# One of eight input tiles in a buffer of its own, at another address, and 31 activation buffers

## The chip, the cores and the metric

The kernel runs on one core of one Trainium2 chip. The metric is the device time of one execution in microseconds. Three executions took 1576.14, 1582.8 and 1582.92 us, a median of 1582.8 us.

## The reference

A trunk of four residual layers over 256 positions with 1024 channels. Layer 0 and 3 mix tokens by a dilated sliding-window attention with three head groups, layer 1 by a gated short convolution, layer 2 by a Conformer convolution module. Every layer ends in a gated convolutional feed-forward block of width 2816. Each sub-layer has a norm before and one after it:

```python
for i in range(DEPTH):
    a = rms_norm(h, mix_norm_pre[i])
    m = mixer[i % 3](a)                    # attention, short conv, conformer, attention
    h = h + rms_norm(m, mix_norm_post[i])
    f = conv_ffn(rms_norm(h, ffn_norm_pre[i]), ffn_w_in[i], ffn_w_conv[i], ffn_w_out[i])
    h = h + rms_norm(f, ffn_norm_post[i])

def conv_ffn(x, w_in, w_conv, w_out):      # w_in 1024 x 5632, w_out 2816 x 1024
    g, v = jnp.split(causal_dwconv(x @ w_in, w_conv), 2, axis=-1)
    return (jax.nn.silu(g) * v) @ w_out
```

All values are float32.

## The kernel before, in words

Channels lie on the 128 partitions and the 256 positions along the free dimension, so an activation of 1024 channels is eight tiles of 128 x 256. A matrix product keeps float32 accuracy by splitting both operands into a high and a low part of the type fp32r: `mm3` (L279 to L282) issues three matmuls for one 128 x 128 block of weights, high weights with the high input, high weights with the low input, low weights with the high input. Each matmul loads 128 columns of weights (the profile's engine PEld) and streams 256 columns of input (engine PE). A column (`column`, L462) is eight such triples, one for each input tile k, into one half of a PSUM bank: 24 matmuls. The first four columns of a stage are issued tile by tile (`ramp`, L433 to L440), since the tiles come one after the other. `value` (L878 to L880) is the attention's other form: there the input tile is the loaded operand, in halves of 128 positions, and the weights stream.

Weights come from HBM in blocks of 1 MB on SP's queue; ScalarE makes the high part (L192) and VectorE the low part (L198), in rings of 11 buffers each. In a feed-forward block 40 columns follow the ramp, and between them stand slabs (`Slabs`, L522): 14 of 24 matmuls each, and eight tails of 24, which multiply gated outputs with the second weight matrix. The short convolution has 20 columns and 192 slab matmuls after its ramp, the Conformer 12 columns, an attention layer 48 columns and 12 values of 48 matmuls. The first column after a ramp carries a hook before tile k = 3 (`if hook and k == 3`, L465): four small matmuls that spread the norm's factor (L324) stand there.

The eight input tiles are made in `boundary` (L341) once for each sub-layer, eight times in all. `hi(k)` takes a buffer by `two()` (L265) and ScalarE writes the high part into its first half (1024 bytes in each partition), `lo(k)` lets VectorE write the low part into the second half. `two()` hands out one of `NACT` equal buffers of 2048 bytes, the pool's tag "act", in turn; nearly all other activations come from the same ring. Ahead of the ring the pool holds a tile of 448 bytes, "gap" (L236), that nothing uses; it moves what comes behind it.

Where the buffers lie in a partition follows from the sizes. Every block of high or low weights begins 32 bytes past a multiple of 512. Every high part and every low part of the ring begins 480 bytes past one (162272 is the ring's first address), so the streamed operand lies 448 bytes, or minus 64, from the loaded one, counted modulo 512. In `value` the operands are swapped, and the distance is plus 64. At the step from a value to a column, and back, one matmul streams from the same place modulo 512 from which the next weights are loaded: distance 0. Such a step is called a crossing below.

The order of the work on each engine is fixed by the order in which the program issues it, and no scheduler changes it.

Of the kernel before, what the change touches and what calls it, by code (L numbers as in the profile page):

```python
# [11 lines left out]
F32R = mybir.dt.float32r  # L12
# [4 lines left out]
P = 128  # L17
D = 1024
T = 256
# [12 lines left out]
BIG = 1e30  # L32
HKF = KF // 2
SLOTS = 11
NACT = 32
PE_TAPS = (13, 13, 13, 15)
SPLIT = 60
FIRST = 10
# [190 lines left out]
def trunk_kernel(ctx: ExitStack, tc: tile.TileContext, xT, pos, params, consts, masks, w8, out):  # L229
# [4 lines left out]
    ap = ctx.enter_context(tc.tile_pool(name="ap", bufs=1))  # L234
    ps = ctx.enter_context(tc.tile_pool(name="ps", bufs=1, space=bass.MemoryType.PSUM))
    ap.tile([P, 112], F32, tag="gap", name="gap")  # L236

    st = Stream(nc, rawp, wp, SLOTS, 3, [w8[i] for i in range(w8.shape[0])])
    for _, _, _, nk, _, cols in plan():
# [15 lines left out]
    def pc(name, k):  # L255
        o, n = PCOLS[name]
        return par[:, o + k:o + k + 1]

    counter = [0]

    def act(dt=F32, tag="act", bufs=NACT, shape=(P, 2, T)):
        counter[0] += 1
        return ap.tile(list(shape), dt, tag=tag, name=f"{tag}{counter[0]}", bufs=bufs)

    def two():  # L265
        t = act(F32R)
        return t[:, 0, :], t[:, 1, :]

    def tmp():
        return act(F32, "tmp", 9, (P, T))  # L270
# [13 lines left out]
    def TT(out, a, b, op):  # L284
        nc.vector.tensor_tensor(out=out, in0=a, in1=b, op=op)  # L285

    def STT(out, a, s, b, op0, op1):
        nc.vector.scalar_tensor_tensor(out=out, in0=a, scalar=s, in1=b, op0=op0, op1=op1)  # L288

    def scaled(out, a, s, b=0.0):  # L290
        nc.scalar.activation(out=out, in_=a, func=AF.Identity, scale=s, bias=b)  # L291

    def perm(a):
        return a.rearrange("p (i j) -> p j i", j=4)
# [22 lines left out]
    def add_eps(out, a, b, eps):  # L317
        STT(out, a, eps * D / P, b, ALU.add, ALU.add)
# [19 lines left out]
    def bc2(a):  # L338
        return a.rearrange("p (s t) -> p s t", s=1).to_broadcast([P, 2, T])

    def boundary(mg, rb, gain, permuted=False):  # L341


        xs = [None] * KD

        def hi(k):
            x = two()
            src = perm(h[k]) if permuted else h[k]
            v = [a.rearrange("p (j i) -> p j i", j=4) for a in x] if permuted else x
            scaled(v[0], src, pc(gain, k))  # L350
            xs[k] = x, v, src

        def lo(k):
            x, v, src = xs[k]
            STT(v[1], src, pc(gain, k), v[0].bitcast(F32), ALU.mult, ALU.subtract)
            xs[k] = x

        sq = []

        def square(q):  # L360
            s = act()
            if permuted:
                for e in range(2):
                    nc.scalar.activation(out=s[:, e, :].rearrange("p (j i) -> p j i", j=4), in_=perm(h[2 * q + e]),
                                         func=AF.Square)
            else:
                nc.scalar.activation(out=s, in_=h2[q], func=AF.Square)
            sq.append(s)

        NP = KD // 2  # L370
        if mg is None:
            for q in range(NP):
                for k in (2 * q, 2 * q + 1):
                    hi(k)
                if q == 0:
                    st.copy()
                for k in (2 * q, 2 * q + 1):
                    lo(k)
                if q == 0:
                    st.diff()  # L380
            for q in range(NP):
                st.copy()
                square(q)
                st.diff()
            st.copy()
            st.diff()
        elif not gain:
            for q in range(NP):
                TT(mg[q], mg[q], bc2(rb), ALU.mult)
                if q:  # L390
                    TT(h2[q - 1], h2[q - 1], mg[q - 1], ALU.add)
                    nc.sync.dma_start(out=out[q - 1], in_=h2[q - 1])
            TT(h2[NP - 1], h2[NP - 1], mg[NP - 1], ALU.add)
            nc.sync.dma_start(out=out[NP - 1], in_=h2[NP - 1])
        else:
            for e in range(2):
                TT(mg[0][:, e, :], mg[0][:, e, :], rb, ALU.mult)
            for e in range(2):
                TT(h[e], h[e], mg[0][:, e, :], ALU.add)
                hi(e)  # L400
            for q in range(1, NP):
                TT(mg[q], mg[q], bc2(rb), ALU.mult)
                lo(2 * q - 2)
                lo(2 * q - 1)
                TT(h2[q], h2[q], mg[q], ALU.add)
                hi(2 * q)
                hi(2 * q + 1)
                square(q - 1)
            lo(KD - 2)
            lo(KD - 1)  # L410
            square(NP - 1)
        if not gain:
            return None, None
        a = sq[0]
        for s in sq[1:]:
            TT(a, a, s, ALU.add)
        acc = tmp()
        add_eps(acc, a[:, 0, :], a[:, 1, :], EPS_RMS)
        return xs, acc
# [137 lines left out]
    def ffn(l, mg, rb):  # L557
# [5 lines left out]
        def gate(last=False):  # L563

            ts = pend.pop(0)
            TT(ts[1], ts[0], ts[1], ALU.mult)
            x = two()
            nc.scalar.copy(out=x[0], in_=ts[1])
            st.diff()
            TT(x[1], ts[1], x[0].bitcast(F32), ALU.subtract)  # L570
            st.copy()
            gs.append(x)
# [41 lines left out]
    def short_conv(l, mg, rb):  # L614
# [10 lines left out]
        for what, k in sc_steps():  # L625
            if what == "col":
# [12 lines left out]
                TT(y, b, rb, ALU.mult)  # L639
                TT(y, y, u, ALU.mult)  # L640
                x = two()
                nc.scalar.copy(out=x[0], in_=y)
                between()
# [558 lines left out]
```

## Time and profile before

| | us |
|---|---|
| median of three executions | 1582.8 |
| profiled execution | 1583.57 |
| its span | 1581.7 |
| TensorE (PE) busy | 1555.7 (98%) |
| VectorE (DVE) busy | 1243.0 (79%) |
| ScalarE (ACT) busy | 925.2 (58%) |

The profiled execution spent 1.87 us outside the span. Each matmul's row has a start and a modelled length; matmuls overlap, so the pace of TensorE is the distance from one start to the next and not the length.

### The profile page before, as it was taken

The numbers are of one execution on the slowest core, as the hardware profiler recorded it, in microseconds if no ns is written. First come the engines' busy times: TensorE is split into PE (matmuls) and PEld (weight loads), VectorE is DVE, ScalarE is ACT, GpSimd is POOL, SyncE is SP. The second block draws the span as 40 slices with busy tenths as digits, with TensorE's granted clock in tenths as the row PEclk, the third lists the DMA queues.
The fourth block names the chain that finished last, engine by engine and source line by source line (L and its number), as shares of the span: only waits on it lengthen the run. The fifth ranks groups of instructions, "written<-read, shape, count | busy, mean of one in ns | idle before, by whom it ended". The sixth has DMA issues, their size and how long they took to land.

```text
span 1581.7 us, 31426 instructions
## 1 busy us (share of the span) xinstructions
PE 1555.7 (98%) x13146; PEld 1520.5 (96%) x13146; DVE 1243.0 (79%) x2177; ACT 925.2 (58%) x1623; POOL 17.9 (1%) x51
## 2 busy tenths in 40 slices
PE   6999999999999999999999999999999999999998
PEld 6999999999999999999999999999999999999997
DVE  4997877697876779889599598786887778588783
ACT  6564655575564566656477666565655445566562
POOL 4000000000000000000000000000000000000000
PEclk9999999999999999999999999999999999999999
DMA  5653543265552644655243136554453434236540
GB/s 218 216 212 131 176 145 108 99 232 204 187 190 100 217 161 162 238 187 184 110 144 124 54 118 239 197 174 153 178 192 138 161 134 160 107 134 237 190 160 28
DMA packets 36718, 256.94 MB, mean 162 GB/s; under 512 B 4320, under 2 KB 4448, under 8 KB 5984
## 3 DMA queue, kind: packets, MB, share of 16 engines
q1 hardware_dynamic: 36288, 254.93, 45.0%
q8 instruction: 103, 1.69, 0.4%
q14 instruction: 39, 0.32, 0.1%
q10 hardware_dynamic: 288, 0.01, 0.0%
HBM read 253.87 MB, written 1.05 MB: 161 GB/s over the span
## 4 chain that ended last, share of the span: by engine, by line
PE 93%; DVE 3%; ACT 1%; POOL 1%; issue 1%; DMA 1%; DVEq 0%; ACTq 0%; POOLq 0%
PE psA L522 17%; PE psB L282 10%; PE psB L280 10%; PE psB L281 10%; PE psA L280 7%; PE psA L281 7%; PE psA L282 7%; PE psA L878 3%; PE psA L880 3%; PE psA L879 3%; PE psB L715 2%; PE psB L926 2%; PE psB L897 2%; PE psA L438 2%; PE psB L915 2%; PE psA L433 2%
## 5 line engine op out<-in xcount | busy, mean ns | idle before, releaser
L198 DVE TENSOR_TENSOR wlo<-raw,whi 128x1024 fp32r<-128x1024 f32 x480 | 580.7, 1221 | 35.3 <-ACT whi L192 34.4
L192 ACT CAST whi<-raw 128x1024 fp32r<-128x1024 f32 x480 | 490.9, 1048 | 23.8 <-DMA raw<-in_w_dram 18.7
L282 PE MATMUL psB<-act,wlo 128*128 128x256 f32 x1392 | 390.7, 281 | 0.0
L280 PE MATMUL psB<-act,whi 128*128 128x256 f32 x1392 | 390.7, 281 | 0.0
L281 PE MATMUL psB<-act,whi 128*128 128x256 f32 x1392 | 390.7, 281 | 0.0
L280 PE MATMUL psA<-act,whi 128*128 128x256 f32 x1040 | 299.2, 288 | 8.0 <-ACT whi L192 7.1
L282 PE MATMUL psA<-act,wlo 128*128 128x256 f32 x1040 | 290.7, 280 | 0.5 <-DVE wlo L198 0.5
L281 PE MATMUL psA<-act,whi 128*128 128x256 f32 x1040 | 290.8, 280 | 0.2
L522 PE MATMUL psA<-act,whi 128*128 128x256 f32 x1536 | 272.9, 281 | 0.0
L281 PEld LDWEIGHTS psB<-act,whi 128*128 128x128 f32 x1392 | 265.0, 190 | 0.0
L282 PEld LDWEIGHTS psB<-act,wlo 128*128 128x128 f32 x1392 | 263.1, 189 | 0.0
L280 PEld LDWEIGHTS psB<-act,whi 128*128 128x128 f32 x1392 | 261.3, 188 | 0.0
L522 PEld LDWEIGHTS psA<-act,whi 128*128 128x128 f32 x1536 | 236.2, 189 | 0.0
L522 PE MATMUL psA<-act,wlo 128*128 128x256 f32 x768 | 215.8, 281 | 0.0
L280 PEld LDWEIGHTS psA<-act,whi 128*128 128x128 f32 x1040 | 196.9, 189 | 12.8 <-ACT whi L192 7.1
L282 PEld LDWEIGHTS psA<-act,wlo 128*128 128x128 f32 x1040 | 197.1, 190 | 0.8 <-DVE wlo L198 0.8
L281 PEld LDWEIGHTS psA<-act,whi 128*128 128x128 f32 x1040 | 197.2, 190 | 0.6 <-DVE act L285 0.5
L291 ACT ACTIVATE tmp<-act,par 128x256 f32<-128x256 f32 x176 | 80.2, 503 | 167.5 <-DVE act L285 167.5
L288 DVE SCALAR_TENSOR_TENSOR tmp<-act,par,tmp 128x255 f32<-128x255 f32 (+1 forms) x352 | 146.7, 480 | 19.7 <-ACT tmp L291 19.7
L522 PEld LDWEIGHTS psA<-act,wlo 128*128 128x128 f32 x768 | 145.2, 189 | 0.0
L285 DVE TENSOR_TENSOR act<-psB,act 128x512 f32<-128x512 f32 (+2 forms) x94 | 58.5, 626 | 89.1 <-PE psB L282 52.2
L878 PE MATMUL psA<-whi,act 128*128 128x256 f32 x384 | 111.0, 289 | 0.0
(124 smaller groups left out, 2116.1 us busy)
## 6 DMA issues: line engine op xcount, KB each, us to landing
raw<-in_w_dram SPq DMA_DIRECT2D x239, 1024.0 KB, 4.8
h<-in_xT_dram SPq DMA_DIRECT2D x4, 256.0 KB, 5.0
raw<-in_w_dram SPq DMA_DIRECT2D x2, 512.0 KB, 5.5
out_dram<-h SPq DMA_DIRECT2D x4, 256.0 KB, 2.0
msk<-in_masks_dram SPq DMA_DIRECT2D x1, 512.0 KB, 9.3
par<-in_params_dram SPq DMA_DIRECT2D x1, 484.0 KB, 10.0
cst<-in_consts_dram SPq DMA_DIRECT2D x1, 132.0 KB, 5.9
par<-in_params_dram ACTq DMA_DIRECT2D x1, 4.0 KB, 2.9
```

The source lines that it names most:

```text
L192: self.nc.scalar.copy(out=hi, in_=raw)
L198: self.nc.vector.tensor_tensor(out=lo, in0=raw, in1=hi.bitcast(F32), op=ALU.subtract)
L280: nc.tensor.matmul(o, lhsT=whi, rhs=x[0], start=first, stop=False)
L281: nc.tensor.matmul(o, lhsT=whi, rhs=x[1], start=False, stop=False)
L282: nc.tensor.matmul(o, lhsT=wlo, rhs=x[0], start=False, stop=last)
L285: nc.vector.tensor_tensor(out=out, in0=a, in1=b, op=op)
L288: nc.vector.scalar_tensor_tensor(out=out, in0=a, scalar=s, in1=b, op0=op0, op1=op1)
L291: nc.scalar.activation(out=out, in_=a, func=AF.Identity, scale=s, bias=b)
L522: nc.tensor.matmul(o, lhsT=a, rhs=b, start=first and i == 0, stop=last and i == 2, skip_group_check=True)
L878: nc.tensor.matmul(oc, lhsT=xh, rhs=whi[:, k % 4, :], start=k == 0, stop=False)
L879: nc.tensor.matmul(oc, lhsT=xh, rhs=wlo[:, k % 4, :], start=False, stop=False)
L880: nc.tensor.matmul(oc, lhsT=xl, rhs=whi[:, k % 4, :], start=False, stop=k == KD - 1)
```

## The change

`boundary` passes the tile's number to `two`, and for k = 3 `two` hands out the two halves of a tile "apart", made once for the whole program between "gap" and the ring. The other seven tiles come from the ring as before, which now has 31 buffers.

```
-NACT = 32
+NACT = 31
+ODD = 3
...
     ap.tile([P, 112], F32, tag="gap", name="gap")
+    apart = ap.tile([P, 2 * T + 32], F32R, tag="apart", name="apart")
...
-    def two():
+    def two(k=None):
+
+        if k == ODD:
+            return apart[:, 16:16 + T], apart[:, 288:288 + T]
         t = act(F32R)
         return t[:, 0, :], t[:, 1, :]
...
         def hi(k):
-            x = two()
+            x = two(k)
```

What this does to addresses: "apart" is 2176 bytes long, 128 more than a ring buffer, and stands ahead of the ring, so all of the ring moves to 96 bytes past a multiple of 512. The low part of tile 3 (1152 bytes into "apart") begins there too. Its high part (64 bytes into "apart") begins at 32, which is 64 bytes past the ring's old place, 64 bytes short of its new one, and the same as the weights' place. The streamed operand of a column now lies plus 64 bytes from the loaded one, modulo 512, and 0 bytes for the high part of tile 3; in a value it is minus 64, and 0.

Every engine issues the same instructions in the same order as before, and every wait of TensorE, VectorE, GpSimd and the queues is the same. Eight waits of ScalarE for its own earlier instructions are different.

## Rows read from the trace of the kernel before

**Rows 1.** The page: busy engines, granted clock in 40 slices.
```profile
PE 1555.7 (98%) x13146; PEld 1520.5 (96%) x13146; DVE 1243.0 (79%) x2177; ACT 925.2 (58%) x1623; POOL 17.9 (1%) x51
...
PEclk9999999999999999999999999999999999999999
```
**Rows 2.** The page's chain of waits, shares of the span by engine.
```profile
PE 93%; DVE 3%; ACT 1%; POOL 1%; issue 1%; DMA 1%; DVEq 0%; ACTq 0%; POOLq 0%
```
**Rows 3.** TensorE's longest waits: total us, times, longest.
```profile
PE psA L280 <- ACT whi L192: 7.1, 1, 7.1
...
PE psA L282 <- DVE wlo L198: 0.5, 1, 0.5
```
**Rows 4.** Four of six stretches: length, each engine's busy time (instructions), granted clock, DMA.
```profile
311.00:484.00 173.00, 173.00 (x1471) 173.00 (x1470) 142.57 (x226) 107.42 (x170) 0.00 (x0) 1.00 0.56 201
503.00:580.00 77.00, 77.00 (x656) 77.00 (x655) 60.27 (x92) 45.76 (x72) 0.00 (x0) 1.00 0.60 217
...
886.00:904.00 18.00, 18.00 (x161) 18.00 (x160) 9.36 (x15) 15.21 (x28) 0.00 (x0) 1.00 0.17 59
...
1397.00:1569.00 172.00, 172.00 (x1462) 172.00 (x1462) 134.34 (x219) 99.70 (x161) 0.00 (x0) 1.00 0.46 166
```
**Rows 5.** Groups by line, 311 to 484 us (feed-forward of layer 0): count, busy, mean ns.
```profile
L280 PE MATMUL psB<-act,whi 128*128 128x256 f32 x288 | 80.9, 281 | 0.0
...
L522 PE MATMUL psA<-act,whi 128*128 128x256 f32 x348 | 61.8, 281 | 0.0
```
**Rows 6.** The same view, 884 to 904.8 us (second half of the Conformer).
```profile
L280 PE MATMUL psB<-act,whi 128*128 128x256 f32 x32 | 8.8, 276 | 0.0
```
**Rows 7.** Timeline of TensorE, first value to column: start us, length, line.
```profile
46.20 0.28 PE L878 MATMUL psA<-whi,act 128*128 128x256 f32 x1
...
46.43 0.28 PE L880 MATMUL psA<-whi,act 128*128 128x256 f32 x1
46.55 0.28 PE L280 MATMUL psA<-act,whi 128*128 128x256 f32 x1
46.67 0.28 PE L281 MATMUL psA<-act,whi 128*128 128x256 f32 x1
46.78 0.28 PE L282 MATMUL psA<-act,wlo 128*128 128x256 f32 x1
46.90 0.28 PE L280 MATMUL psA<-act,whi 128*128 128x256 f32 x1
```
**Rows 8.** The same, column to value, 45 starts later.
```profile
52.00 0.28 PE L878 MATMUL psA<-whi,act 128*128 128x256 f32 x1
...
52.79 0.28 PE L879 MATMUL psA<-wlo,act 128*128 128x256 f32 x1
```
**Rows 9.** The same, value to column again.
```profile
57.10 0.28 PE L878 MATMUL psA<-whi,act 128*128 128x256 f32 x1
...
57.33 0.28 PE L880 MATMUL psA<-whi,act 128*128 128x256 f32 x1
57.44 0.28 PE L280 MATMUL psA<-act,whi 128*128 128x256 f32 x1
57.56 0.28 PE L281 MATMUL psA<-act,whi 128*128 128x256 f32 x1
...
57.80 0.28 PE L280 MATMUL psA<-act,whi 128*128 128x256 f32 x1
```
**Rows 10.** Groups by line, attention of layer 0, 62 to 287 us.
```profile
L281 PE MATMUL psA<-act,whi 128*128 128x256 f32 x340 | 94.5, 278 | 0.1
...
L879 PE MATMUL psA<-wlo,act 128*128 128x256 f32 x144 | 40.1, 279 | 0.0
```
**Rows 11.** The same, attention of layer 3, 1114 to 1366 us.
```profile
L281 PE MATMUL psA<-act,whi 128*128 128x256 f32 x381 | 105.7, 277 | 0.1
...
L879 PE MATMUL psA<-wlo,act 128*128 128x256 f32 x192 | 53.5, 278 | 0.0
```

## The prediction

> **What bounds the kernel now.** The page comes first: TensorE is busy for 98% of the span [rows 1] and carries 93% of the chain of waits [rows 2]. Its longest wait for another engine is one of 7.1 us at the start, and for weights from VectorE it waits 0.5 us in all [rows 3]. So the time is the number of matmuls times the distance from one start to the next. [...]
>
> The next view is the busy time by stretches. It also counts matmuls that began up to 0.28 us before the stretch, so 0.28 us are added. From 311 to 484 us, in the feed-forward of layer 0, it is (173.00 + 0.28) / 1471 = 117.8 ns from start to start; from 886 to 904 us, in the Conformer, (18.00 + 0.28) / 161 = 113.5 ns [rows 4]. These are the same instruction forms with no wait among them. The groups by line show it too: a mean length of 281 ns in the one stretch and 276 ns in the other [rows 5, 6]. I call them the long and the short pace. Short convolution, 503 to 580 us, and layer 3's feed-forward, 1397 to 1569 us, run at the long one [rows 4]; so do the two feed-forwards in between.
>
> The timeline shows where the pace changes without a wait. At 46 us a value ends and a column begins, a crossing in the sense given above: starts lie 0.12 us apart until 46.78 us, then 46.90 us begins a run [rows 7] that reaches 52.00 us after 45 starts, 5.10 / 45 = 113.3 ns [rows 8]. At 52.00 us a column gives way to a value, again over a distance of 0, and the pace stays: 46.90 to 52.79 us is 52 starts, 5.89 / 52 = 113.3 ns, so this crossing costs under 2 ns. At 57.44 us a value gives way to a column, and the pace turns from short (57.10 to 57.44 us, 3 starts) to long (57.44 to 57.80 us, 3 starts in 0.36 us) [rows 9]. So at equal addresses both paces hold themselves, and what turns one into the other, with no wait near, is a step in the distance between streamed and loaded addresses.
>
> **The change, part by part.** Nothing is added, removed or moved in order, so the only direct terms are buffers and addresses.
>
> *31 buffers.* The ring turns over one buffer sooner, but tile 3 no longer takes one. No wait of TensorE or VectorE changes, and eight of ScalarE change toward its own, earlier work, which is done when it gets there. Cost 0; ScalarE, busy 58% [rows 1], covers it, and eight waits of even one cast could not add 8 us.
>
> *Tile 3's high part.* In each column the distance now goes 64, 0, 64, 0, 64 around tile 3: two crossings where there was none. Columns whose input comes from `boundary`: 160 in four feed-forwards, 20, 12, and 96 in two attentions, with 24 values beside them, some 310. I read the crossing as a push that ends the long pace, as at 46.78 us, and leaves the short one, as at 52.00 us. Per matmul that is 117.8 - 113.3 = 4.5 ns. The terms:
> - Feed-forward: 40 columns, 14 slabs and 8 tails of 24 are 1488 matmuls, four times 5952, 26.8 us. Slabs have no odd tile; they keep the pace of the column before, as the short one was kept for 45 starts across two columns [rows 7, 8].
> - Short convolution: 480 + 192 = 672, 3.0 us. Conformer's first half: 288, 1.3 us.
> - Attention: mean lengths of 278 and 279 ns in layer 0, between 276 and 281, make 0.4 of 3 x 340 column matmuls and 0.6 of 3 x 144 value matmuls long; 277 and 278 in layer 3 make 0.2 of 3 x 381 and 0.4 of 3 x 192 [rows 10, 11]. That is 408 + 259 + 229 + 230 = 1126. Transposes break these columns up, and tile 3 comes late in each, so half: 563, 2.5 us.
>
> Together 33.6 us. Against it 310 x 2 crossings at under 2 ns [rows 8], 1.2 us at most, of which I take 1.0. Next in line is VectorE: 142.57 of 173 us in a feed-forward [rows 4] become 142.57 of 166.4, 86%, still under TensorE; I take 1.0 us for low weights that come late, which is twice what all such waits are now [rows 3]. Net 31.6 us, from the profiled execution's 1583.6 us: 1552 us. That execution lies 0.8 us above the median.
>
> *The new distance, plus 64.* A value runs at it now, at 279 ns on average in layer 0 against the columns' 278 [rows 10]. Both paces exist there too, the short one from 52.00 to 57.44 us [rows 8, 9]. I give the steady pace at it no price; the bounds are the two paces.
>
> *A steady distance of 0.* The first four columns of each stage use tile 3's high part eight times in a row against weights at distance 0. The trace has only single steps of it: 0.12 us between starts at 46.55 to 46.78 us [rows 7], like the long pace, and under 0.115 us at 52.00 us [rows 8]. Over 8 stages x 8 matmuls the difference is 64 x 4.5 ns = 0.3 us either way, which I leave out.
>
> **The rivals.**
>
> *No effect.* The pace is set by something other than addresses, and the long one stays. For it: 1471 starts in a row keep it through columns and slabs [rows 4, 5]; and a crossing can leave a pace as it is [rows 8]. Against it: the two others above turn it. It gives 1583 to 1586 us, the upper end if 310 x 2 crossings cost 4 ns each, the difference between 0.12 and 0.116 us, 2.5 us. [...]
>
> *Half of it.* The push works in both directions, so every second column is long, as a value's end made one pace short at 46.78 us and the other long at 57.44 us [rows 7, 9]. Half of 33.6 us, 16.8, less 1.0: about 1568 us.
>
> *Slower.* The crossing out of the short pace decides: in each column tile 3 throws it into the long pace, as at 57.44 us, and nothing brings it back. Its place is the two attentions, where the short pace has 0.6 x 1020 + 0.4 x 432 + 0.8 x 1143 + 0.6 x 576 = 2045 matmuls, 9.2 us, and crossings at 4 ns add 2.5 us: 1595 us. From 60% of those matmuls on it is slower by more than a measurement can miss ((7.9 - 2.5) / 9.2 us).
>
> **How the numbers follow.** The outcome hangs on two questions: does the push end the long pace (at 46.78 us it did), and does it spare the short one (at 52.00 us it did, at 57.44 us it did not). I give the forecast 0.35, half of it 0.17, no effect 0.23, slower 0.25. A measurement can tell 0.5%, 7.9 us, from no change: below 1574.9 us is faster, above 1590.7 us slower. The first two cases are faster, 0.52; no effect is within, 0.23; the rest slower, 0.25. The forecast's own range is 1547 (the other half of the attention, 2.5 us, and no price for crossings and VectorE) to 1561 us (a third of the feed-forward stays long, 8.9 us). The range reaches to the other cases: 1546 to 1596 us.
>
> **What would show it.** Right: the stretches of the feed-forwards show a mean length of 276 ns where 281 stood, some 1488 matmuls in 168.6 us, and slabs in step with the columns; within the first column behind a ramp the starts close up to 0.113 us from tile 3 on. Wrong: 281 ns in the feed-forwards, or a mean above it. Half: a mean near 278.5 ns, with columns that alternate. The slower rival shows in the attentions, with lengths of 281 ns where 277 and 278 stood. If TensorE then waits for low weights by several us, VectorE was nearer than I put it.

## The result, and the profile after

The changed kernel takes 1593.33 us (median of four executions, 1592.70 to 1593.88). The kernel before took 1582.86 us beside it (four executions, 1576.14 to 1583.16). The ratio is 1.0081, with a 95% interval of 1.0056 to 1.0105. Ratios below leave out one execution of experiment 8, which lasted 8732.95 us. The forecast of 1552 us was wrong; the time lies where the rival "slower" put it, at 1595 us.

The profiled execution took 1593.88 us, with a span of 1592.0 us. Three rows of the page of the changed kernel answer to [rows 1], and its shares of the chain of waits to [rows 2]:

```profile
PE 1565.4 (98%) x13146; PEld 1529.7 (96%) x13146; DVE 1243.6 (78%) x2177; ACT 924.9 (58%) x1623; POOL 18.5 (1%) x51
...
PEclk9999999999999999999999999999999999999999
...
PE 95%; DVE 2%; POOL 1%; ACT 1%; DMA 1%; issue 0%; DVEq 0%; ACTq 0%; POOLq 0%
```

The same 13146 matmuls are busy for 9.7 us more at the same granted clock (0.997 on average, 0.996 before), while VectorE and ScalarE stand where they were. The two waits of TensorE of [rows 3] have not grown (total us, times, longest; a line stands up to five further down than before). Another at the start, for ScalarE, went from 4.8 to 5.5 us:

```profile
PE psA L285 <- ACT whi L193: 7.0, 1, 7.0
PE psB L1093 <- ACT act L1084: 5.5, 1, 5.5
...
PE psA L287 <- DVE wlo L199: 0.5, 1, 0.5
```

So most of the loss must be in the distance between starts. The stretches of [rows 4], moved along by what the program is late there (length, busy time and count of PE, PEld, DVE, ACT, POOL, clock, DMA):

```profile
311.00:484.00 173.00, 173.00 (x1472) 173.00 (x1471) 142.01 (x230) 107.76 (x170) 0.00 (x0) 1.00 0.55 196
503.00:580.00 77.00, 77.00 (x657) 77.00 (x656) 59.73 (x95) 43.30 (x65) 0.00 (x0) 1.00 0.56 205
888.00:906.00 18.00, 18.00 (x153) 18.00 (x154) 8.72 (x17) 15.26 (x28) 0.00 (x0) 1.00 0.04 5
1407.00:1579.00 172.00, 172.00 (x1463) 172.00 (x1462) 134.64 (x219) 99.69 (x162) 0.00 (x0) 1.00 0.47 166
```

In the feed-forwards and the short convolution the counts are those of before: the long pace has stayed, 1472 matmuls against 1471 in 173 us. In the Conformer 161 have become 153: what ran at the short pace there now runs at the long one. The groups by line say the same for the Conformer's second half, 887 to 907 us, where [rows 6] had 276 ns, and for the attentions of layer 0 (62 to 290 us) and layer 3 (1122 to 1376 us), where [rows 10, 11] had 278 and 277 ns for the columns and 279 and 278 for the values (count, busy, mean ns):

```profile
L285 PE MATMUL psB<-act,whi 128*128 128x256 f32 x22 | 6.2, 280 | 0.0
```
```profile
L286 PE MATMUL psA<-act,whi 128*128 128x256 f32 x303 | 84.8, 280 | 0.1
...
L884 PE MATMUL psA<-wlo,act 128*128 128x256 f32 x126 | 35.3, 280 | 0.0
```
```profile
L286 PE MATMUL psA<-act,whi 128*128 128x256 f32 x338 | 94.6, 280 | 0.1
...
L884 PE MATMUL psA<-wlo,act 128*128 128x256 f32 x168 | 47.1, 280 | 0.0
```

The timeline of TensorE shows what happens inside an attention's column (start us, length; "apart" is tile 3):

```profile
110.28 0.28 PE L287 MATMUL psA<-act,wlo 128*128 128x256 f32 x1
...
110.95 0.28 PE L287 MATMUL psA<-act,wlo 128*128 128x256 f32 x1
111.07 0.28 PE L285 MATMUL psA<-apart,whi 128*128 128x256 f32 x1
111.19 0.28 PE L286 MATMUL psA<-apart,whi 128*128 128x256 f32 x1
111.31 0.28 PE L287 MATMUL psA<-apart,wlo 128*128 128x256 f32 x1
111.43 0.28 PE L285 MATMUL psA<-act,whi 128*128 128x256 f32 x1
...
112.01 0.28 PE L287 MATMUL psA<-act,wlo 128*128 128x256 f32 x1
```

From 110.28 to 110.95 us there are 6 starts in 0.67 us, 112 ns each: the short pace. From 111.07 to 111.43 us there are 3 in 0.36 us, 120 ns. From 111.43 to 112.01 us there are 5 in 0.58 us, 116 ns, and from there to its end the column keeps the long pace. Tile 3 has thrown the column out of the short pace, and nothing has brought it back.

The engines issue the same instructions in the same order, so both traces can be laid over each other matmul by matmul, and the time from the start of one to the start of another compared:

| stretch (starts) | before, us | after, us | |
|---|---|---|---|
| each of four feed-forwards from the hook on (1478) | 174.08 | 174.07 | 0.0 |
| short convolution from the hook on (662) | 77.97 | 77.97 | 0.0 |
| layer 0: first columns, then the attention | 39.45 + 223.41 | 39.83 + 226.16 | +3.1 |
| layer 3: the attention | 246.74 | 250.45 | +3.7 |
| two attentions' output columns | 11.45 + 11.56 | 11.90 + 12.01 | +0.9 |
| Conformer, second half | 21.08 | 21.95 | +0.9 |
| six ramps with the column behind each, up to the hook | | | +1.3 |

These are 9.9 of the 10.3 us between the two profiled executions. Most of the rest lies in the small matmuls between the Conformer's two halves, where in both traces the granted clock is at 0.5 for 3.4 us: 10.11 us became 10.68. The 0.4 us of the first columns lie in a stretch that holds the longer wait for ScalarE, so they are not clearly tile 3's or the ring's.

### The profile page after: what moved, and what is told of

The parts are those of the page before. It is cut to its first block, busy times and chain, and to the rows that moved or that the text cites. A ratio compares the mean times of both kernels' runs of the same rounds, so it can differ in the third digit from the quotient of the medians.

```text
span 1592.0 us, 31425 instructions
## 1 busy us (share of the span) xinstructions
PE 1565.4 (98%) x13146; PEld 1529.7 (96%) x13146; DVE 1243.6 (78%) x2177; ACT 924.9 (58%) x1623; POOL 18.5 (1%) x51
## 3 DMA queue, kind: packets, MB, share of 16 engines
HBM read 253.87 MB, written 1.05 MB: 160 GB/s over the span
## 4 chain that ended last, share of the span: by engine, by line
PE 95%; DVE 2%; POOL 1%; ACT 1%; DMA 1%; issue 0%; DVEq 0%; ACTq 0%; POOLq 0%
PE psA L527 17%; PE psB L286 10%; PE psB L285 10%; PE psB L287 10%; PE psA L285 8%; PE psA L286 7%; PE psA L287 7%; PE psA L883 3%; PE psA L884 3%; PE psA L885 3%; PE psB L720 2%; PE psB L902 2%; PE psB L931 2%; PE psA L443 2%; PE psB L920 2%; PE psA L438 2%
## 5 line engine op out<-in xcount | busy, mean ns | idle before, releaser
L286 PE MATMUL psB<-act,whi 128*128 128x256 f32 x1230 | 344.7, 280 | 0.0
L285 PE MATMUL psB<-act,whi 128*128 128x256 f32 x1230 | 344.2, 280 | 0.0
L287 PE MATMUL psB<-act,wlo 128*128 128x256 f32 x1230 | 343.3, 279 | 0.0
L285 PE MATMUL psA<-act,whi 128*128 128x256 f32 x918 | 265.3, 289 | 7.9 <-ACT whi L193 7.0
L527 PE MATMUL psA<-act,whi 128*128 128x256 f32 x1536 | 272.9, 280 | 0.0
L287 PE MATMUL psA<-act,wlo 128*128 128x256 f32 x918 | 257.5, 280 | 0.5 <-DVE wlo L199 0.5
L286 PE MATMUL psA<-act,whi 128*128 128x256 f32 x918 | 257.7, 281 | 0.2
L527 PEld LDWEIGHTS psA<-act,whi 128*128 128x128 f32 x1536 | 234.4, 188 | 0.0
L285 PEld LDWEIGHTS psB<-act,whi 128*128 128x128 f32 x1230 | 231.4, 188 | 0.0
L286 PEld LDWEIGHTS psB<-act,whi 128*128 128x128 f32 x1230 | 231.0, 188 | 0.0
L287 PEld LDWEIGHTS psB<-act,wlo 128*128 128x128 f32 x1230 | 230.3, 187 | 0.0
L527 PE MATMUL psA<-act,wlo 128*128 128x256 f32 x768 | 214.3, 279 | 0.0
L285 PEld LDWEIGHTS psA<-act,whi 128*128 128x128 f32 x918 | 173.5, 189 | 12.7 <-ACT whi L193 7.0
L286 PEld LDWEIGHTS psA<-act,whi 128*128 128x128 f32 x918 | 173.6, 189 | 0.6 <-DVE act L290 0.5
L287 PEld LDWEIGHTS psA<-act,wlo 128*128 128x128 f32 x918 | 172.9, 188 | 0.9 <-DVE wlo L199 0.8
L527 PEld LDWEIGHTS psA<-act,wlo 128*128 128x128 f32 x768 | 143.6, 187 | 0.0
L911 ACT ACTIVATE act<-act,tiny 128x512 f32<-128x512 f32 x64 | 46.4, 725 | 110.6 <-DVE tiny L909 110.6
```

Of the source, the lines that this page charges most:

```text
L285: nc.tensor.matmul(o, lhsT=whi, rhs=x[0], start=first, stop=False)
L286: nc.tensor.matmul(o, lhsT=whi, rhs=x[1], start=False, stop=False)
L287: nc.tensor.matmul(o, lhsT=wlo, rhs=x[0], start=False, stop=last)
L527: nc.tensor.matmul(o, lhsT=a, rhs=b, start=first and i == 0, stop=last and i == 2, skip_group_check=True)
```

## The experiments

Each is the changed kernel or the kernel before with one edit. "Distance" is streamed minus loaded address, modulo 512, as in the prediction; it is minus 64 in the kernel before, plus 64 in the changed one, and 0 for tile 3's high part. Three theories stand behind experiments 4 to 7; T, D, S and C stand in the expectations themselves. L: what counts is where a step of the distance lands; a step that lands on minus 64 ends the long pace, one that lands on plus 64 ends the short one. Z: what counts is that the distance is 0 at some matmul of the column. A: what counts is the alignment of the buffers, and not their distance. Unless said otherwise a stretch of 320 to 470 us lies in the feed-forward of layer 0; in the kernel before it holds 1276 matmuls, and 1326 would be the short pace throughout:

```profile
320.00:470.00 150.00, 150.00 (x1276) 150.00 (x1275) 127.09 (x202) 93.79 (x145) 0.00 (x0) 1.00 0.59 211
```

**1. The ring's move alone.** Tile 3 comes from the ring again; "apart" stays in its place, unused.

```
-            x = two(k)
+            x = two()
```

> All eight input tiles from the ring, which stays at its new place, plus 64 bytes from the weights modulo 512; 31 buffers. Theory T (tile 3's crossing throws the short pace into the long one, and nothing brings it back): the crossing is gone, so the short pace comes back in the attentions, the ramps and the second half of the Conformer: 1583 us. Theory D (at plus 64 the ring's own distance loses the short pace): 1593 us, as with the whole change, with a mean length of 281 ns in the second half of the Conformer.

Measured: 1589.26 us, ratio 1.0045 (1.0029 to 1.0060), between the 1583 us of T and the 1593 us of D. The feed-forward is long as before:

```profile
320.00:470.00 150.00, 150.00 (x1276) 150.00 (x1275) 127.47 (x203) 93.62 (x145) 0.00 (x0) 1.00 0.58 210
```

Laid over the kernel before, layer 0's attention is 1.4 us longer and layer 3's 1.5, the output columns 0.9, the Conformer's second half 0.8 and the ramps 1.2. So about 6 of the 10.5 us come with the ring at plus 64 with no odd tile at all. Of the other 4, 3.6 are tile 3's, in the attentions: they lose 2.9 us here and 6.5 in the changed kernel (both without the first columns). The small matmuls at the low clock (0.5), which lose 0.6 us in the changed kernel, lose none here.

**2. The tile alone.** The ring goes back to minus 64, since "apart" is now 2560 bytes long; tile 3's high part stays at distance 0, its low part at minus 64.

```
-    apart = ap.tile([P, 2 * T + 32], F32R, tag="apart", name="apart")
+    apart = ap.tile([P, 2 * T + 128], F32R, tag="apart", name="apart")
...
-            return apart[:, 16:16 + T], apart[:, 288:288 + T]
+            return apart[:, 16:16 + T], apart[:, 384:384 + T]
```

> Tile 3 in a buffer of its own with its high part at distance 0, and the ring at its old place, minus 64. T: in the attentions each column turns long at tile 3, 1590 to 1592 us; the Conformer's second half and the first four output columns of the attentions, which have no such tile, keep the short pace. D: 1583 us, attentions as before.

Measured: 1559.64 us, ratio 0.9852 (0.9837 to 0.9867). T and D expected no gain, and both missed. The push of the forecast is there, at a ring that stands at minus 64. Its first column behind a ramp in layer 0, tile 3 and then the end:

```profile
311.46 0.36 PE L285 MATMUL psA<-apart,whi 128*128 128x256 f32 x1
311.66 0.28 PE L286 MATMUL psA<-apart,whi 128*128 128x256 f32 x1
311.78 0.28 PE L287 MATMUL psA<-apart,wlo 128*128 128x256 f32 x1
311.90 0.28 PE L285 MATMUL psA<-act,whi 128*128 128x256 f32 x1
...
312.61 0.28 PE L285 MATMUL psA<-act,whi 128*128 128x256 f32 x1
...
313.29 0.28 PE L285 MATMUL psA<-act,whi 128*128 128x256 f32 x1
```

From 311.66 to 311.90 us two starts take 0.24 us; from 312.61 to 313.29 us six take 0.68 us, 113 ns. Ahead of the hook this column's starts are 118 ns apart. In the four feed-forwards, the short convolution and the Conformer's first half, six stages, it is the same: long up to tile 3, short within nine starts from it. The pace stays short to the end of the layer, in the slabs too (2299 of 2304 slab distances):

```profile
320.00:470.00 150.00, 150.00 (x1317) 150.00 (x1316) 129.63 (x207) 96.72 (x151) 0.00 (x0) 1.00 0.59 211
```

It is 1317 and not 1326, because each column pays for its step to 0 and back: the starts around tile 3 are 119, 118, 118, 122, 116 and 114 ns apart, 27 ns over six short ones. The attentions gain nothing, +0.5 and +0.8 us.

**3. 31 buffers alone**, in the kernel before.

```
-NACT = 32
+NACT = 31
```

> Only 31 buffers in place of 32, every address as before modulo 512. Both theories: 1583 us, within 0.5%. If it is slower by several us, the shorter ring costs by itself.

Measured: 1583.55 us, ratio 0.9999 (0.9990 to 1.0008). The buffers cost nothing. One thing in its trace is a warning: here too the Conformer's second half is long, 21.95 us, at minus 64. So which pace that stretch falls into is not the distance's alone, and I count its 0.9 us in the changed kernel as not explained.

**4. Alignment.** In the kernel before, 32 bytes ahead of the weights move weights and activations alike: everything lies on a multiple of 64 bytes, and the distance between them does not change. One other distance does: the hook streams an identity matrix from the constants, which stay where they were.

```
+    cp.tile([P, 8], F32, name="pad")
```

> The kernel before with all weights and activations moved by 32 bytes together, so that they begin on multiples of 64 bytes; their distance modulo 512 is unchanged. If only the distance counts (D and T): 1583 us, paces of 113.3 and 117.8 ns. [...]

Measured: 1567.21 us (1561.46 to 1571.22), ratio 0.9887 (0.9867 to 0.9907), and not 1583 us. A would have shown as a pace shorter than the short one, and there is none: it is 113.34 and 117.78 ns as before. The gain is whole feed-forwards that fall into one or the other. Of layer 0 to 3:

```profile
320.00:470.00 150.00, 150.00 (x1276) 150.00 (x1275) 127.11 (x203) 93.75 (x145) 0.00 (x0) 1.00 0.58 211
610.00:760.00 150.00, 150.00 (x1326) 150.00 (x1325) 130.60 (x208) 98.33 (x153) 0.56 (x5) 1.00 0.61 218
925.00:1075.00 150.00, 150.00 (x1326) 150.00 (x1325) 131.78 (x209) 98.70 (x153) 0.00 (x0) 1.00 0.60 217
1395.00:1545.00 150.00, 150.00 (x1275) 150.00 (x1275) 122.28 (x198) 89.33 (x141) 0.00 (x0) 1.00 0.50 181
```

Behind the hook layers 1 and 2 are short and stay so for all 1478 starts, 6.56 us less each; layers 0 and 3 stay long. In these two kernels without an odd tile a feed-forward's pace is settled at the hook, and not by the pace ahead of it: here layers 1 and 2 are long ahead of the hook, and in the kernel before three of the four feed-forwards are short ahead of it (113.3 to 113.4 ns) and long behind it (117.8 ns). So at one distance, minus 64 bytes, a stage can fall into either pace with no step at all. Whether it is the hook's own distance or the 32 bytes as such that turned layers 1 and 2 isn't shown. This kernel's executions differ by up to 10 us; one feed-forward more or less is 6.6, which is also how far the lowest execution of the kernel before (1576.14 us) lies under its median. That this is the reason there was not traced.

**5 and 6. Other steps that land on minus 64.** The layout of experiment 2, with tile 3's high part at plus 64, and at minus 128, instead of 0.

```
+            return apart[:, 32:32 + T], apart[:, 384:384 + T]
```
```
+            return apart[:, 112:112 + T], apart[:, 384:384 + T]
```

> Ring at its old place (minus 64 modulo 512); tile 3's high part at plus 64 instead of 0. Theory Z (it is distance 0 that pushes: streamed and loaded operand in the same place): no push, the feed-forwards stay at 117.8 ns, 1583 to 1592 us. Theory L (it is the landing on minus 64, from any other distance, that leaves the short pace behind): as with tile 3 at 0, feed-forwards at about 114 ns, 1560 us.

> Ring at its old place; tile 3's high part 64 bytes on the other side, at minus 128. Z: no push, 1583 to 1592 us. L: 1560 us. If it lands near 1560 us while plus 64 does not, the direction of the step counts.

Measured: 1557.27 us, ratio 0.9845 (0.9818 to 0.9872), and 1563.49 us, ratio 0.9884 (0.9857 to 0.9912). First the one, then the other:

```profile
320.00:470.00 150.00, 150.00 (x1322) 150.00 (x1321) 130.06 (x207) 97.04 (x152) 0.00 (x0) 1.00 0.59 213
```
```profile
320.00:470.00 150.00, 150.00 (x1315) 150.00 (x1315) 130.28 (x206) 96.89 (x150) 0.00 (x0) 1.00 0.59 211
```

Both end the long pace in the feed-forwards, and in neither is an operand of a column at distance 0. Z falls: it isn't 0 that counts. From plus 64 the push is less sure: in five of six stages the first column stays long behind tile 3, and only the second column's tile 3 ends the long pace. So with the ring at minus 64 an odd tile at any of three distances ends the long pace. The price differs too: the feed-forward takes 168.15 us from plus 64, 168.59 from 0 and 168.84 from minus 128, against 167.55 without a step (experiment 8), which is 15, 26 and 32 ns for each of 40 columns.

**7. The mirror.** The ring at plus 64, as in the changed kernel, with tile 3's high part at minus 64.

```
-            return apart[:, 16:16 + T], apart[:, 288:288 + T]
+            return apart[:, 0:T], apart[:, 288:288 + T]
```

> Ring at its new place (plus 64) as in the changed kernel; tile 3's high part at minus 64, so that a triple goes 64, -64, 64, -64, 64. L: the columns land on plus 64, where no step has yet brought the short pace: 1593 us. Z: there is no distance 0 in a column: the ring's cost alone, 1589 us.

Measured: 1588.39 us, ratio 1.0044 (1.0026 to 1.0062), level with experiment 1. The feed-forward stays long:

```profile
320.00:470.00 150.00, 150.00 (x1277) 150.00 (x1276) 127.24 (x202) 93.83 (x146) 0.00 (x0) 1.00 0.59 210
```

A step that lands on plus 64 does not end the long pace, from minus 64 here or from 0 in the changed kernel. But tile 3 does end the short one, as L had it. One of the attention's columns:

```profile
46.29 0.28 PE L285 MATMUL psA<-act,whi 128*128 128x256 f32 x1
...
47.31 0.28 PE L285 MATMUL psA<-apart,whi 128*128 128x256 f32 x1
...
47.67 0.28 PE L285 MATMUL psA<-act,whi 128*128 128x256 f32 x1
...
48.37 0.28 PE L285 MATMUL psA<-act,whi 128*128 128x256 f32 x1
```

From 46.29 to 47.31 us nine starts take 1.02 us, 113 ns; from 47.67 to 48.37 us six take 0.70 us, 117 ns. That the time is level with experiment 1 all the same, and not at the 1593 us of L, is two effects that cancel: the attentions are 1.4 and 2.1 us longer than before, against 1.4 and 1.5 with no odd tile, since their columns run longer (117.3 ns on average, against 116.5 and 116.1 in experiment 1) and their values shorter (114.8 and 114.7 ns, against 116.2 and 116.0).

The traces hold 273 columns that read tile 3 and have no hook. Counted by the pace ahead of tile 3 and the pace at the column's end:

| kernel | ring at | tile 3's high part at | long ahead: turn short | short ahead: turn long |
|---|---|---|---|---|
| before | -64 | -64 | 0 of 205 | 0 of 68 |
| experiment 2 | -64 | 0 | 16 of 20 | 0 of 253 |
| experiment 5 | -64 | 64 | 21 of 40 | 0 of 233 |
| experiment 6 | -64 | -128 | 11 of 21 | 0 of 252 |
| experiment 1 | 64 | 64 | 0 of 245 | 0 of 28 |
| changed | 64 | 0 | 0 of 263 | 10 of 10 |
| experiment 7 | 64 | -64 | 0 of 250 | 23 of 23 |

So at minus 64 tile 3 ends the long pace, though not every time, and never the short one; at plus 64 it ends the short pace every time, and never the long one. Without an odd tile no column turns. Tile 3's distance is left and come back to twice in a column, so which of the steps does it, out or back, no run tells apart. The misses at minus 64 are in part all eight Conformer columns behind other matmuls (L715 in the kernel before) in experiments 5 and 6; why is open.

**8. One step in each stage, from a second copy.** The ring at minus 64 and all of tile 3 in it; a second copy of its high part, at distance 0, is read only by the ramp and the first column behind it in feed-forwards, short convolution and Conformer. ScalarE writes one copy more in these six stages. The core of the edit, against the changed kernel:

```
-    apart = ap.tile([P, 2 * T + 32], F32R, tag="apart", name="apart")
+    apart = ap.tile([P, 384], F32R, tag="apart", name="apart")[:, 16:16 + T]
...
+            if k == ODD and not permuted:
+                v = apart, x[1]
...
+        if not permuted:
+            scaled(xs[ODD][0], h[ODD], pc(gain, ODD))
...
+    def odd(xs):
+        return xs[:ODD] + [(apart, xs[ODD][1])] + xs[ODD + 1:]
...
-                    column(xs, o, hook)
+                    column(odd(xs) if hook else xs, o, hook)
```

> Ring at its old place; a second copy of tile 3's high part at distance 0, used only in the ramp and in the one column after the hook, in feed-forwards, short convolution and Conformer; none in the attentions; one more cast on ScalarE for each of six stages. If one landing is enough and the pace then keeps itself: feed-forwards at 113.3 ns without the 27 ns that each further crossing cost, 4 x 6.5 + 2.9 + 1.2 = 30 us under before, 1553 us. If the pace does not keep itself over columns and slabs without a crossing in each: 1570 us or more.

Measured: 1554.8 us, ratio 0.9827 (0.9808 to 0.9846). It is the fastest kernel of the study, 28 us under the kernel before:

```profile
320.00:470.00 150.00, 150.00 (x1326) 150.00 (x1325) 130.17 (x206) 97.28 (x151) 0.00 (x0) 1.00 0.60 216
```

The steps of one tile in one column are enough, and the extra copy isn't what does it, since experiment 2 has none and turns at the same place. Every feed-forward then runs all its 1478 starts at 113.36 ns, 6.5 us less in each, and the short convolution 2.9 us less. Again the Conformer's second half fell into the long pace, +0.8 us.

**9 to 12. A steady distance.** The kernel before with another length of "gap" (in floats), so that all of the ring stands at distance 0, 256, minus 128 and minus 32.

```
-    ap.tile([P, 112], F32, tag="gap", name="gap")
+    ap.tile([P, 128], F32, tag="gap", name="gap")
```

with 64, 96 and 120 in the three others.

> The kernel before, its ring moved so that all streamed inputs lie at distance 0 from the weights modulo 512 and no tile stands apart. Theory S (the two paces, 113.3 and 117.8 ns, hold themselves at any distance, and the distance only decides which one a start falls into): both paces and no third, feed-forwards at one of the two, 1555 to 1592 us. Theory C (streams in the same place delay each other): a longer pace than 117.8 ns, over 1600 us.

> The same with all streamed inputs at plus 256, as far as they can be modulo 512. S: both paces, 1555 to 1592 us. C: the short pace everywhere, 1545 to 1555 us.

> The same with all streamed inputs at minus 128. S: both paces, 1555 to 1592 us. If distance counts only modulo 128, as distance 0: the time of that kernel within 2 us.

> The kernel before with all streamed inputs at minus 32, half way between distance 0 (120.0 ns from start to start) and minus 64 (113.3 or 117.8 ns). If the pace changes smoothly with the distance, between these: 117 to 120 ns in the feed-forwards, 1585 to 1605 us. [...]

Measured: 1615.96 us, ratio 1.0226 (1.0175 to 1.0276); 1616.26 us, 1.0228 (1.0176 to 1.0279); 1603.10 us, 1.0144 (1.0094 to 1.0195); 1597.75 us, 1.0088 (1.0059 to 1.0117). The stretch in the four, in this order:

```profile
320.00:470.00 150.00, 150.00 (x1253) 150.00 (x1252) 129.56 (x212) 92.80 (x145) 0.00 (x0) 1.00 0.56 198
```
```profile
320.00:470.00 150.00, 150.00 (x1253) 150.00 (x1252) 129.55 (x211) 92.77 (x146) 0.00 (x0) 1.00 0.56 197
```
```profile
320.00:470.00 150.00, 150.00 (x1267) 150.00 (x1266) 130.66 (x210) 94.18 (x146) 0.00 (x0) 1.00 0.58 204
```
```profile
320.00:470.00 150.00, 150.00 (x1270) 150.00 (x1269) 129.25 (x208) 93.40 (x145) 0.00 (x0) 1.00 0.57 206
```

(150.00 + 0.28) us over the counts give 119.9, 119.9, 118.6 and 118.3 ns. So the ring's place alone changes the pace, with the same instructions, the same order and a granted clock of 1.00. At 0 and at 256 it is the same, and there is only one pace: a feed-forward takes 177.36 us in both. S misses at 0, 256 and minus 128, where a third pace stands; C holds at 0 and misses at 256. Minus 128 is 13 us from 0, so the distance doesn't count modulo 128 alone, and minus 32 lies between 0 and minus 64 and equals neither, as its expectation had it: 118.3 ns, and 1597.75 us.

## Why the prediction was wrong, step by step

**What bounds the kernel: right.** Nearly all of the change of time, some 9.5 of 10.3 us, is a change of pace of TensorE at a granted clock of 1.00. Of the rest, 0.6 us lie at the low clock (0.5) and 0.4 us beside a longer wait at the start.

**31 buffers at no cost: right** (experiment 3: ratio 0.9999).

**The step that failed** is "I read the crossing as a push that ends the long pace, as at 46.78 us", applied to a ring at plus 64. At 46.78 us [rows 7] the distance steps from plus 64, the value's, to minus 64, the column's. In the changed kernel a column steps from 0 to plus 64. I took from the row that a step was made, and left out where it landed. I also let it spare the short pace, and at plus 64 it ended that in 10 of 10 columns. Experiments 2, 5 and 6 show the push at a ring that stands at minus 64, from three sides; the changed kernel and experiment 7 show none at plus 64. The 31.1 us of the sum in feed-forwards, short convolution and Conformer (26.8, 3.0 and 1.3) became 0. The row of the other direction was there: at 52.00 us [rows 8] the step lands on plus 64, and all that it showed was that the short pace can survive it. No row showed a long pace ended by a step onto plus 64. Nor is the step from value to column the same as tile 3's: of nine such steps in the two attentions of the kernel before, from 46 us on, seven turn the long pace short and two, one at 57.44 us [rows 9], the short pace long; the eight steps back onto plus 64 leave either pace as it is. In a ring at minus 64 tile 3's steps never ended the short pace.

**"The new distance, plus 64 … I give the steady pace at it no price": wrong by about 6 us** (experiment 1). Both paces exist there, as I said. But ramps, output columns and parts of the attentions that ran short now run long: of the attentions' 87 columns 28 in place of 68 are short at tile 3. Why a stage falls into the long pace more often at plus 64 isn't settled.

**Crossings: under 2 ns each was right in one case and too low in another.** In the long pace at plus 64 they cost nothing: 40 columns with two crossings each, 174.07 us against 174.08. In the short pace at minus 64 a pair costs 15 to 32 ns, so 40 columns cost 1.05 us (experiment 2), as against the 0.16 us of my price.

**Attention: wrong in sign.** I took 2.5 us for it as a gain; it lost 6.8 us with the first columns of layer 0. Even where the push works, experiment 2 gains nothing there: 68 of the 87 columns counted in the attentions ran short in the kernel before already, and those pay for the steps.

**The rival "slower" had a mechanism that the runs show, and its time by luck**: tile 3 throws the attention's columns into the long pace. But it put 9.2 us on that and 2.5 on the crossings: the attentions lost 6.5 us, of which 2.9 come with the ring's move, without any tile at another distance, and the crossings cost nothing in the long pace. The remaining 3.1 us of the table, in output columns, ramps and the Conformer, stood in none of the cases.

**Where the forecast's gain would have been**: had the ring kept its place, the same odd tile would have given 1559.6 us, 8 us above the forecast: the attentions lost 1.4 us where I had a gain of 2.5, and the crossings in the feed-forwards cost 4.2 us where I had 1.0 for all of them. The 1.0 us for late low weights was near: at the short pace such waits come to 0.9 us in experiment 2 and 1.2 us in experiment 8, against 0.5 us before. "Apart" is 128 bytes longer than a ring buffer, and everything behind it moved by that, which is what turned a gain of 23 us into a loss of 10.

## What to carry to other kernels

When a buffer's size changes, work out the place of everything behind it before reasoning about the buffer itself, and change one address at a time. Where an engine is busy for 98% of the time, read the distances from start to start by stretch: two paces of one instruction form at one clock are worth a search, here 28 us. When a row is taken as a pattern for another place, write down all that it holds (from where, to where, in which direction), and look for a row that matches all of it.

## What the runs showed of the hardware

- The pace of these matmuls (128 columns of weights loaded, 256 columns streamed, each with its own weights, at a granted clock of 1.00) went with the distance of the two addresses, counted modulo 512: from 320 to 470 us it was 119.9 ns at 0 and at 256, 118.6 at minus 128 and 118.3 at minus 32, and at plus or minus 64 it was 113.3 or 117.8. Experiments 2 and 9, with the same instructions at 1559.6 and 1616.0 us, show that the places of TensorE's own two operands change its pace. In the changed kernel the two waits of [rows 3] are as they were, 7.0 and 0.5 us against 7.1 and 0.5. Which part of the memory or of the engine makes the difference no run showed.
- At minus 64 two paces (113.3 and 117.8 ns) held themselves for as long as a stage lasts, 1478 starts, through slabs and columns (experiment 4). At plus 64 the long one did (174.07 us for 1478 starts in the changed kernel); the short one held for up to 118 starts in a row (experiment 1, attention of layer 3). At 0 and 256 only one was seen (177.36 us for 1478 starts).
- With the ring at minus 64, the steps of one tile turned the long pace into the short one, from 0, from plus 64 and from minus 128 (16 of 20, 21 of 40 and 11 of 21 columns without a hook), and the first column of a stage was enough for it in all six stages of experiment 8. With the ring at plus 64 the same kind of steps turned the short pace into the long one, in 10 of 10 and 23 of 23 columns. Why the direction goes with the ring's place, why a step between value and column can turn either pace, and why the Conformer's second half goes its own way (experiments 3 and 8), is open.
